# Batched matrix product: the last 2 MB load as two DMAs, and the first store waiting for the first of them

## The chip, the cores and the metric

The kernel runs on one NeuronCore of a Trainium2 chip. The metric is the device time of one execution in microseconds (us), the median of several executions. All DMAs of this kernel are issued by SyncE (SP), so they stand in one queue; TensorE (PE) multiplies, VectorE (DVE) casts the inputs to bf16, ScalarE (ACT) moves results out of PSUM, GpSimd (POOL) only waits at the end.

## The reference

```python
batch, m, k, n = 16, 512, 512, 512
a: (batch, k, m) float32      b: (batch, k, n) float32

def reference(a, b):
    return np.matmul(a.transpose(0, 2, 1), b).astype(np.float32)
```

Sixteen products of 512 x 512 matrices, the first of each stored transposed. The inputs are 33.55 MB, the output is 16.78 MB, and each byte crosses between HBM and SBUF once.

## The kernel before

**Tiling.** The 16 products are taken in 8 pairs. A load (one for a, one for b) brings a whole pair, 2 MB: the 128 partitions hold 64 partitions of each of the two products, and each partition holds R = 8 consecutive rows of its matrix, one contiguous run of 16 KB. Four such tiles (`x0` to `x3`, NX = 4) are used in rotation: load n goes into `x[n % 4]`, even n is a, odd n is b. The first pair is fetched in smaller pieces (256 KB, 768 KB, 1 MB for each of a and b). Counting by whole loads, the last two are n = 14 (a of pair 7) and n = 15 (b of pair 7).

**Casts.** DVE turns each tile into bf16 in two halves (v = 0 and v = 1, RV = 4 rows of each partition, tiles `abf0/1` and `bbf0/1`), line 109. For v = 0 it first waits until the load has landed (line 108, semaphore `s_x[n % 4]`). After the second half it raises `s_in`, which tells SP that the tile is free.

**Matmuls.** PE runs a loop over the pairs (line 136): for each half v, it waits for two casts and issues 32 matmuls into four PSUM tiles (line 147). ACT copies the finished PSUM tiles into an output tile `o` (line 172) and raises `s_out` once per pair (line 177). There are 7 output tiles for 8 pairs, so the results of nearly all pairs can stay in SBUF until they are stored.

**The order on SP.** SP's program is written out by hand, and an instruction that waits holds up everything behind it:

1. the six small loads of pair 0;
2. loads n = 2 to 15 (line 80); from n = 4 on each waits for `s_in`, that is, for the casts that free its tile;
3. line 83, a wait until load 14 has landed:

```python
n = 2 * pairs - 2
nc.sync.wait_ge(s_x[n % NX], 16 * (n // NX + 1))
```

4. the stores of pairs 0 to 6 (line 86), each behind a wait for `s_out` of its pair; 2 MB each, in runs of 8 KB (one partition and one of the two products);
5. after a barrier at the end of the block, the store of pair 7 (line 184).

So no store is issued until the loads are nearly over: the inputs stream in first, then the outputs stream out. POOL waits for the stores of pairs 0 to 6, and the program ends when the store of pair 7 has landed.

Of the kernel before, what the change touches and what calls it, by code (L numbers as in the profile page):

```python
# [8 lines left out]
def kernel(  # L9
# [6 lines left out]
    nc = tc.nc  # L16
# [11 lines left out]
    R = K // Q  # L28
    V = 2
    RV = R // V  # L30
    T = M // P
    H = T // 2
    pairs = batch // G
    in_v = [x.rearrange("(pair g) (q r) m -> pair (g q) r m", g=G, r=R) for x in (a, b)]
# [8 lines left out]
    NX = 4  # L43
# [10 lines left out]
    x_ts = [pool.tile([P, R, M], f32, name=f"x{j}") for j in range(NX)]  # L54
# [4 lines left out]

    s_x = [tc.alloc_semaphore(f"s_x{j}") for j in range(NX)]  # L60
    s_f = [tc.alloc_semaphore(f"s_f{j}") for j in range(2)]
    s_o0 = tc.alloc_semaphore("s_o0")
    s_o = tc.alloc_semaphore("s_o")
    s_in = tc.alloc_semaphore("s_in")
# [6 lines left out]
    with tc.tile_critical(no_gpsimd_drain=True):  # L71
# [5 lines left out]
        for n in range(2, 2 * pairs):  # L77
            if n >= NX:
                nc.sync.wait_ge(s_in, n - NX + 1)
            nc.sync.dma_start(x_ts[n % NX][:], in_v[n % 2][n // 2]).then_inc(s_x[n % NX], 16)  # L80

        n = 2 * pairs - 2
        nc.sync.wait_ge(s_x[n % NX], 16 * (n // NX + 1))
        for i in range(pairs - 1):
            nc.sync.wait_ge(s_out, i + 1)
            nc.sync.dma_start(out_v[i], o_ts[i % NO][:]).then_inc(s_o if i else s_o0, 16)
# [11 lines left out]
        for i in range(1, pairs):  # L98
            for v in range(V):
                if i == 1 and v == 0:  # L100
                    nc.vector.wait_ge(s_mm, G * H)
                if i > 1 and v == 0:
                    nc.vector.wait_ge(s_v, G * (i - 1))
                if i > 1 and v == 1:
                    nc.vector.wait_ge(s_mm, G * H * i)
                for n in (2 * i, 2 * i + 1):
                    if v == 0:
                        nc.vector.wait_ge(s_x[n % NX], 16 * (n // NX + 1))
                    nc.vector.tensor_copy(  # L109
                        out=(bbf_ts if n % 2 else abf_ts)[v][:],  # L110
                        in_=x_ts[n % NX][:, v * RV:(v + 1) * RV, :],
                    ).then_inc(s_cast, 1)
                    if v == V - 1:

                        nc.vector.memset(dve_done[:, n:n + 1], 0.0).then_inc(s_in, 1)  # L115
# [99 lines left out]
```

## Time and profile before

| quantity | value |
|---|---|
| median of 5 runs | 123.85 us (123.58 to 124.2) |
| the profiled execution's own time | 123.61 us |
| its span, first to last instruction | 121.9 us |
| PE busy | 63.6 us (52%) |
| DVE busy | 37.9 us (31%) |
| ACT busy | 32.2 us (26%) |
| one 2 MB load, issue to landing, median (a / b) | 12.1 / 15.9 us |
| one 2 MB store, issue to landing, median | 25.1 us |
| HBM read / written | 33.55 / 16.78 MB |

The time of the profiled execution is 1.7 us longer than its span, and 0.24 us shorter than the median. A 2 MB transfer that is issued into a full queue lands long after its issue, since it stands behind others: the last two rows but one are waiting times more than transfer times.

Besides the engines' instructions the trace holds a record of every DMA packet, with its start, its duration and its size. Packets of the 2 MB loads are 16 KB and take 611 ns each; packets of the stores are 8 KB and take 309 ns each. The packets run on 16 DMA engines (called rings below). When a DMA is through on a ring, the ring writes 4 bytes to its semaphore; the DMA has landed when all 16 of these writes are made.

### The profile page before, as it was taken

To read this page: it belongs to the slowest core of one execution; us is meant where nothing else is said; L and a number is where in the kernel's file an instruction comes from. 1 tells how busy PE (TensorE), PEld (TensorE's weight loads), DVE (VectorE), ACT (ScalarE), POOL (GpSimd) and SP (SyncE) were. 2 spreads that over 40 slices of the span, in tenths; PEclk is the share of its full clock that TensorE was granted. 3 is DMA by queue.
4 is the path that set the end of the run, shared out by engine and by line. 5 is a ranking of instruction groups with operands and counts; after the bars stand their busy time and mean duration, and the time that the engine had idled before them with its cause. 6 is when DMAs were issued, how large, how long until landed. Compare 5 with 4: busy or idle time off the path is not lost. (4 is left out here: it accounts for less than half of the span.)

```text
span 121.9 us, 1208 instructions
## 1 busy us (share of the span) xinstructions
PE 63.6 (52%) x480; PEld 35.7 (29%) x480; DVE 37.9 (31%) x48; ACT 32.2 (26%) x41; POOL 0.2 (0%) x4
## 2 busy tenths in 40 slices
PE   0006928739979659979919929936991000000000
PEld 0002403226546335636516606612550000000000
DVE  0052070294494091484265447419000000000000
ACT  4000330510660930190560380190048000000000
POOL 0000000000000000000000000000000000000000
PEclk9999995999999995999999999995899855555555
DMA  3999999999999999999999999999999999999994
GB/s 92 383 415 428 457 430 430 430 430 430 430 436 436 430 430 430 430 430 430 430 430 430 436 430 430 430 358 425 430 428 428 422 430 428 428 428 430 430 430 202
DMA packets 5056, 50.33 MB, mean 413 GB/s; under 512 B 448, under 2 KB 448, under 8 KB 960
## 3 DMA queue, kind: packets, MB, share of 16 engines
q1 hardware_dynamic: 5056, 50.33, 97.8%
HBM read 33.55 MB, written 16.78 MB: 413 GB/s over the span
## 5 line engine op out<-in xcount | busy, mean ns | idle before, releaser
L147 PE MATMUL ps<-bbf,abf 64*128 64x512 bf16 x448 | 52.8, 393 | 15.4 <-PEq L142 15.4
L147 PEld LDWEIGHTS ps<-bbf,abf 64*128 64x128 bf16 x448 | 31.7, 112 | 36.6 <-issue 22.0
L172 ACT COPY o<-ps 128x1024 f32<-128x1024 f32 x28 | 26.3, 1026 | 42.5 <-PE ps L147 42.5
L109 DVE CAST abf<-x 128x2048 bf16<-128x2048 f32 x14 | 17.1, 1224 | 17.2 <-PE ps L147 11.9
L109 DVE CAST bbf<-x 128x2048 bf16<-128x2048 f32 x14 | 17.1, 1224 | 16.7 <-DMA x<-in_b_dram 16.7
L127 PE MATMUL ps<-bbf,abf 128*128 128x512 bf16 x32 | 10.8, 512 | 12.8 <-PEq L125 12.8
L127 PEld LDWEIGHTS ps<-bbf,abf 128*128 128x128 bf16 x32 | 4.1, 133 | 19.0 <-issue 18.0
L166 ACT COPY o<-ps 128x1024 f32<-128x1024 f32 x4 | 4.1, 1013 | 18.4 <-PE ps L127 18.4
L93 DVE CAST abf<-x 128x2048 bf16<-128x2048 f32 x2 | 2.5, 1226 | 12.0 <-PE ps L127 6.1
L93 DVE CAST bbf<-x 128x2048 bf16<-128x2048 f32 x2 | 2.4, 1224 | 1.5 <-DMA x<-in_b_dram 1.5
L177 ACT ACTIVATE done<-done 1x1 uint32<-1x1 uint32 x8 | 1.6, 197 | 0.0
L166 ACT ACT_TABLE_LOAD x1 | 1.3, 1283 | 0.9 <-SPq L71 0.9
L115 DVE MEMSET done<- 1x1 f32 x14 | 0.8, 59 | 0.0
L97 DVE MEMSET done<- 1x1 f32 x2 | 0.1, 59 | 0.0
L199 POOL MEMSET const-bfloat16-1.0<- 128x1 bf16 x1 | 0.1, 103 | 0.0
L199 POOL MEMSET const-uint8-127<- 128x1 uint8 x1 | 0.1, 102 | 0.0
L199 POOL MEMSET const-float32-0.0<- 128x1 f32 x1 | 0.1, 100 | 0.2 <-issue 0.2
L199 POOL MEMSET const-float32-1.0<- 128x1 f32 x1 | 0.1, 99 | 0.0
## 6 DMA issues: line engine op xcount, KB each, us to landing
out_dram<-o SPq DMA_DIRECT2D x8, 2048.0 KB, 25.1
x<-in_a_dram SPq DMA_DIRECT2D x7, 2048.0 KB, 12.1
x<-in_b_dram SPq DMA_DIRECT2D x7, 2048.0 KB, 15.9
x<-in_a_dram SPq DMA_DIRECT2D x1, 1024.0 KB, 8.2
x<-in_b_dram SPq DMA_DIRECT2D x1, 1024.0 KB, 10.1
x<-in_a_dram SPq DMA_DIRECT2D x1, 768.0 KB, 4.4
x<-in_b_dram SPq DMA_DIRECT2D x1, 768.0 KB, 6.2
x<-in_a_dram SPq DMA_DIRECT2D x1, 256.0 KB, 2.7
```

What stands on the lines that cost most here:

```text
L93: nc.vector.tensor_copy(out=bf_ts[0][:], in_=x_ts[j][:, u * RV:(u + 1) * RV, :]).then_inc(s_cast, 1)
L97: nc.vector.memset(dve_done[:, j:j + 1], 0.0).then_inc(s_in, 1)
L109: nc.vector.tensor_copy(out=(bbf_ts if n % 2 else abf_ts)[v][:], in_=x_ts[n % NX][:, v * RV:(v + 1) * RV, :],).then_inc(s_cast, 1)
L115: nc.vector.memset(dve_done[:, n:n + 1], 0.0).then_inc(s_in, 1)
L127: mm = nc.tensor.matmul(ps_ts[0][h][:, t % 2, :], a_m[:, r, t], bbf_ts[0][:, r, :], start=(r == 0), stop=(r == RV - 1),)
L147: mm = nc.tensor.matmul(ps_ts[g][h][:, t % 2, :], a_m[:, t], bbf_ts[v][rows, r, :], start=(v == 0 and r == 0), stop=(v == V - 1 and r == R ...
L166: nc.scalar.copy(out=o_ts[0][:, g, 2 * h:2 * h + 2, :], in_=ps_ts[0][h][:]).then_inc(s_ev[h], 1)
L172: ev = nc.scalar.copy(out=o_ts[i % NO][:, g, 2 * h:2 * h + 2, :], in_=ps_ts[g][h][:])
L177: nc.scalar.memzero(act_done[:, i:i + 1]).then_inc(s_out, 1)
L199: nc = _bacc.Bacc("TRN2", target_bir_lowering=False, num_devices=1)
```

## The change

Load 15 is split into two DMAs of 1 MB. Each partition's 16 KB run becomes two of 8 KB: the first DMA brings rows 0 to 3 of each partition, which the cast v = 0 reads, and signals a new semaphore `s_h`; the second brings rows 4 to 7, which the cast v = 1 reads, and signals `s_x[3]`. SP waits for `s_h` in place of the landing of load 14 before it issues the first store. DVE waits for `s_h` before the first half-cast of load 15, and for `s_x[3]` before the second. Nothing else differs.

```diff
+    s_h = tc.alloc_semaphore("s_h")
...
-            nc.sync.dma_start(x_ts[n % NX][:], in_v[n % 2][n // 2]).then_inc(s_x[n % NX], 16)
-
-        n = 2 * pairs - 2
-        nc.sync.wait_ge(s_x[n % NX], 16 * (n // NX + 1))
+            src, x = in_v[n % 2][n // 2], x_ts[n % NX]
+            if n < 2 * pairs - 1:
+                nc.sync.dma_start(x[:], src).then_inc(s_x[n % NX], 16)
+            else:
+                nc.sync.dma_start(x[:, 0:RV, :], src[:, 0:RV, :]).then_inc(s_h, 16)
+                nc.sync.dma_start(x[:, RV:R, :], src[:, RV:R, :]).then_inc(s_x[n % NX], 16)
+
+        nc.sync.wait_ge(s_h, 16)
...
-                    if v == 0:
+                    last = n == 2 * pairs - 1
+                    if last and v == 0:
+                        nc.vector.wait_ge(s_h, 16)
+                    if last and v == 1 or not last and v == 0:
                         nc.vector.wait_ge(s_x[n % NX], 16 * (n // NX + 1))
```

## The prediction

> **What bounds the kernel now.** I read the page's slices first, then the DMA queue, then the waits of SP, then short windows around the step from loads to stores, and last the packet records there.
>
> ```profile
> span 121.9 us, 1208 instructions
> ...
> PE   0006928739979659979919929936991000000000
> ...
> DMA  3999999999999999999999999999999999999994
> GB/s 92 383 415 428 457 430 430 430 430 430 430 436 436 430 430 430 430 430 430 430 430 430 436 430 430 430 358 425 430 428 428 422 430 428 428 428 430 430 430 202
> ...
> q1 hardware_dynamic: 5056, 50.33, 97.8%
> ```
>
> The DMA engines are busy in every slice, 97.8% of the span in all, while PE stops two thirds of the way through. The kernel is one stream of packets: 78 us of loads, 39 us of stores, a start of 2 us and a tail of 1.3 us. The engines matter only where they keep the stream from being fed. The one slice that falls clearly short is the 27th, 358 GB/s, about 79 to 82 us: the step from loads to stores, where the change works.
>
> ```profile
> SPq L80 <- DVE done L115: 43.8, 10, 8.5
> SPq L210 <- DMA out_dram<-o: 26.4, 1, 26.4
> ...
> SPq L86 <- DMA x<-in_a_dram: 10.6, 1, 10.6
> SPq L86 <- ACT done L177: 3.2, 1, 3.2
> ```
>
> In this view of SP's waits (line, who is waited for, us, times, longest) the third row is the wait that the change replaces: SP holds the first store until load 14 has landed.
>
> ```profile
> 12.00:78.00 66.00, 50.78 (x392) 29.42 (x392) 31.73 (x41) 23.24 (x30) 0.00 (x0) 0.95 1.01 432
> 78.50:81.50 3.00, 1.87 (x18) 0.95 (x14) 0.00 (x0) 2.85 (x4) 0.00 (x0) 1.00 0.93 350
> 82.00:120.00 38.00, 8.53 (x64) 4.28 (x64) 3.25 (x5) 4.29 (x7) 0.00 (x0) 0.65 1.01 428
> ```
>
> In these windows the last figure is GB/s: 432 in the loads, 428 in the stores, 350 for 3 us between. At 430 that stretch would carry (430 - 350) x 3.0 = 240 KB more, 0.56 us of streaming. The semaphore writes give the loss more sharply. On the mean of the 16 rings, fourteen whole loads end 4.86 us apart, the stores 4.90, but load 15 ends 5.23 after load 14: 0.37 us lost. On the ring that is last, load 14 ends at 76.28 and load 15 at 81.37, 5.09 apart: 0.22 lost. The packets show where: the 16 KB packets that begin between 78.7 and 79.9 take up to 1,138 ns for 611. None is lost later: the first 8 KB store packet of a ring follows its last load packet at once, 80.94 on the earliest ring, and takes 309 ns like all others.
>
> **The change part by part**, against the profiled execution (span 121.9, time 123.61; the median is 0.24 above it, and I add the sum to the median).
>
> Two halves for one load: 8 packets of 16 KB per ring become 16 of 8 KB. The row for 8 KB loads is in the first pair, whose two 1 MB halves end 2.45 us apart; two are 4.90 for 4.86: +0.04 us.
>
> One more issue on SP: an issue of a whole load lasts 0.33 us, and the last begins at 65.63. The second half would be issued by 66.3, and its data are due 2.45 us after 76.28, so 12 us of queued loads cover it. Without that cover it would cost its 0.33 us.
>
> DVE and what follows: the first half-cast of load 15 begins at 81.75, 0.38 us after the landing. With the first half landing at 76.28 + 2.45 = 78.73 it can begin at about 79.1; the second half lands about 81.2, close to where the whole did. PE's last pair can then start up to 2.5 us sooner than 83.27, and the last store be issued up to that much before 94.11. This is worth nothing: that store's packets start only when six stores have drained, at 120.57 - 4.90 = 115.7. If the last pair came late instead, the cover is 115.7 - 94.11, some 21 us.
>
> The later wait: this is the term that decides.
>
> ```profile
> 76.60 12.48 SPq L86 DMA_DIRECT2D out_dram<-o  x7
> ...
> L86 SPq DMA_DIRECT2D out_dram<-o x7: 403/560/5146, 76.6 to 84.5; - x7
> ```
>
> These are the timeline and the line's own view (duration in ns, shortest, median, longest). The first store is issued at 76.60, 0.32 after load 14's last semaphore write; the sixth takes 5.1 us because the queue takes no more. After the change SP waits for 78.73 and issues at 78.73 + 0.32 = 79.05, 2.45 later. All seven stores of line 86, the barrier and the store of line 184 stand behind that wait. Five stores then go out at about 0.56 us each, far faster than the 4.9 us in which one drains, so all depends on whether the first is in time.
>
> When do the rings run dry? Without any slowdown they end the second half one load after load 14: 75.71 + 4.90 = 80.62 on the first ring, 81.18 on the last. From issue to a store's first packet there is no direct row, since all stores so far were issued into a full queue.
>
> The bound below is the kernel's first load, issued into empty rings at 0.94: its first packets begin between 1.96 and 2.25, so 1.02 to 1.31. The store would be there at 80.07 to 80.36, before any ring runs dry: no gap. The bound above is the first store itself: issued at 76.60, and the first packets of load 15 that take longer begin between 78.75 and 79.27, 2.15 to 2.67 later. If that is the moment when a store's work reaches the rings, it now does so at 81.20 to 81.72, after they have run dry. A dry ring also has to fill again: the first two packets of the kernel take 0.27 us more than 2 x 84 ns on the mean of the rings. The first store then runs at full rate from 81.47 to 81.99, where before it did on the last ring from 81.37: +0.10 to +0.62 us.
>
> I take the upper bound. It is the same kind of DMA at the same place in the stream, while the first load is another kind at another place. The end of the kernel is set by the last ring, so I take the upper part of the 0.10 to 0.62 and say +0.50. The slowdown goes with it, for the loads would be over before a store touches them; that is in the sum already, which compares with 81.37. The 0.04 lies before the dry spell. Sum: 123.85 + 0.50 = 124.35.
>
> Two rules of the Trainium skill bear on this. "DMA: Bandwidth & Descriptors", section "Bandwidth", gives 341 GB/s for a 1 MB load (one issued by GpSimd) and wants no smaller ones; by it the two halves would cost 2 x 1.05 MB / 341 = 6.1 us for 4.9, an estimate of +1.3, 125.1 us. The trace's halves, which stand in a stream of others, show no such loss. The same page, section "Latency and other measured facts", puts the first byte of a DMA issued by SP at about 0.6 us after issue; by that the store would be in time at 79.7, and the sum would be no worse than +0.04, 123.9.
>
> **The rivals.**
>
> *Seamless, and nothing comes of it.* The store arrives as quickly as the first load did. For it: the rows of the first load, and 0.3 to 1.1 us of margin. The slowdown either stays, since its cause (store reads beside the last load writes) is only moved, +0.04; or it goes on the last ring, 0.04 - 0.22 = -0.18. 123.67 to 123.9.
>
> *Seamless, and the slowdown goes on all rings* (faster). For it: it is the only loss in the stream, it comes after the stores are issued, and only there. On the mean of the rings it is 0.37, by the windows 0.56; less 0.04 it is 0.33 to 0.52, and the time 123.33 to 123.52, say 123.43. Against it: the last ring loses only 0.22, and all rings must be finished. But the profiled execution is 0.24 shorter than the median, and a longer slowdown in ordinary ones would fit that.
>
> *The slowdown stays and the gap is added* (slower). The stores reach the rings late, the last rings still write loads and are slowed by 0.22 to 0.37, and the dry ones fill up behind: +0.62 + 0.37 = +1.0, 124.85. It decides as soon as the way from issue to packet is over 2.1 us (81.18 - 79.05). Against it: overlap and gap can hardly both be long on one ring.
>
> **How the numbers follow.** About 0.3% (0.37 us) is what a measurement of this kernel can tell from no change. The forecast, a gap, has 0.50; its own range is +0.10 to +0.80, 123.95 to 124.65, and I give 0.43 of it to slower and 0.07 to same. Seamless without effect has 0.19: 0.16 same, 0.03 faster. Seamless with gain has 0.24: 0.23 faster, 0.01 same. Gap and slowdown has 0.07, slower. Together faster 0.26, same 0.24, slower 0.50. The time is that of the forecast, 124.35. The range leaves out the tips of the two outer cases: 123.4 to 124.95.
>
> **What would show it.** A gap: in the profile after, the slice near 81 us falls below 358 GB/s, and a window of half a microsecond there carries less than the 197 of 80.00 to 80.50 before; load packets stay at 611 or 309 ns to their end, and the first store packets begin later than 81.4. Seamless: the stores' packets follow the second half without a break, and then either some of its packets are long (no effect) or none (gain). The halves are right if they end 2.45 us apart. The forecast is wrong if the first store packet begins less than 1.6 us after its issue, for then no ring runs dry; the chances are wrong if anything outside 78 to 83 us moves the end.

## The result, and the profile after

| | before | after |
|---|---|---|
| median, many runs of both | 123.93 us (86 runs) | 123.61 us (44 runs) |
| ratio, 95% interval | | 0.9965 [0.9954, 0.9977] |
| the profiled execution's own time | 123.61 us | 123.73 us |
| its span | 121.9 us | 122.0 us |

By the ratio the kernel is faster by 0.35%, some 0.43 us; the two medians lie 0.32 us apart. The forecast was slower by 0.50 us: it was wrong.

The page's slices and its DMA queue, after:

```profile
span 122.0 us, 1209 instructions
...
PE   0006919289989949829969928989900000000000
...
DMA  3999999999999999999999999999999999999993
GB/s 98 373 429 430 470 430 430 430 430 430 430 430 430 430 430 430 430 430 430 430 430 430 430 430 419 419 424 430 427 427 430 427 430 430 430 430 424 430 430 132
...
q1 hardware_dynamic: 5200, 50.33, 97.6%
```

The 27th slice, 358 GB/s before, now has 424. The step from loads to stores can hardly be seen any more. The 144 packets more are 128 for the halved load and 16 semaphore writes.

SP's waits after (line, who is waited for, us, times, longest), then the timeline around the step (start, duration, engine, line, operation):

```profile
SPq L83 <- DVE done L123: 43.5, 9, 9.0
SPq L218 <- DMA out_dram<-o: 26.6, 1, 26.6
...
SPq L91 <- DMA x<-in_b_dram: 12.6, 1, 12.6
```

```profile
79.38 10.09 SPq L91 DMA_DIRECT2D out_dram<-o  x7
79.39 1.23 DVE L117 CAST bbf<-x 128x2048 bf16<-128x2048 f32 x1 [0.87 <-DMA x<-in_b_dram]
...
81.06 7.21 PE L155 MATMUL ps<-bbf,abf 64*128 64x512 bf16 x64 [0.35 <-PEq L150]
...
90.72 3.64 SPq L192 DMA_DIRECT2D out_dram<-o  x1
```

SP now waits for a piece of b, and the first store is issued at 79.38, 2.78 us later than before. The cast of the first half begins at once, PE's last pair 2.2 us sooner, and the last store is issued 3.4 us sooner.

```profile
12.00:78.00 66.00, 51.88 (x391) 28.91 (x391) 31.59 (x41) 23.22 (x30) 0.00 (x0) 0.92 1.01 431
78.50:81.50 3.00, 2.65 (x27) 1.46 (x23) 2.00 (x3) 2.51 (x3) 0.00 (x0) 1.00 1.01 429
82.00:120.00 38.00, 6.27 (x58) 3.68 (x54) 1.12 (x2) 4.62 (x7) 0.00 (x0) 0.64 1.01 426
```

These are the windows of the prediction on the kernel after, the last figure GB/s again. The middle one carries 429 where it carried 350. A part of that difference comes from how such a window counts; the experiment with the late store alone shows how much.

The packet records say the same without the windows' edges. Times are in us. A load ends on a ring with its semaphore write; "last ring" is the latest of the 16 writes, and "load 15 after load 14" the time from one end to the next:

```
                                          before   after
load 14 ends, last ring                    76.28   76.60
load 15 after load 14, mean of the rings    5.23    4.91  (2.45 + 2.45)
load 15 after load 14, last ring            5.09    4.91
the 8 stores, last ring                    39.20   39.20
from the last packet to the span's end      1.30    1.27
```

No packet of the halves takes longer than 309 ns, and the first store packets follow without a break, from 80.55 on: 1.17 us after their issue. No ring ran dry. That the profiled execution after is nevertheless 0.12 longer is the first row: its last ring was 0.32 later from the start of the kernel on, which took back the 0.18 won at the step. One ring's late start is carried through to the end, and it differs from execution to execution; so the gain must be read from the many runs.

### The profile page after: what moved, and what is told of

Same layout as the page of the kernel before. It is cut to its first block, busy times and chain, and to the rows that moved or that the text cites. A ratio compares the mean times of both kernels' runs of the same rounds, so it can differ in the third digit from the quotient of the medians.

```text
span 122.0 us, 1209 instructions
## 1 busy us (share of the span) xinstructions
PE 63.5 (52%) x480; PEld 35.4 (29%) x480; DVE 38.2 (31%) x48; ACT 32.1 (26%) x41; POOL 0.2 (0%) x4
## 4 chain that ended last, share of the span: by engine, by line
DMA 59%; DVE 6%; issue 3%; ACT 3%; SPq 3%; ACTq 0%
DMA x<-in_b_dram 53%; DMA out_dram<-o 6%; ACT o L180 3%; DVE bbf L117 3%; DVE abf L117 3%; SPq L77 1%; SPq L75 1%; SPq L74 1%; SPq L83 0%; DVE done L123 0%; ACTq L72 0%; SPq L218 0%; SPq L72 0%
## 5 line engine op out<-in xcount | busy, mean ns | idle before, releaser
L155 PE MATMUL ps<-bbf,abf 64*128 64x512 bf16 x448 | 54.5, 401 | 11.8 <-PEq L150 11.8
L135 PE MATMUL ps<-bbf,abf 128*128 128x512 bf16 x32 | 9.0, 444 | 13.0 <-PEq L133 13.0
```

What stands on the lines that cost most here:

```text
L135: mm = nc.tensor.matmul(ps_ts[0][h][:, t % 2, :], a_m[:, r, t], bbf_ts[0][:, r, :], start=(r == 0), stop=(r == RV - 1),)
L155: mm = nc.tensor.matmul(ps_ts[g][h][:, t % 2, :], a_m[:, t], bbf_ts[v][rows, r, :], start=(v == 0 and r == 0), stop=(v == V - 1 and r == R ...
```

## The experiments

All are compared with the kernel before on the same chip. Two theories were to be told apart at first: that the later issue of the first store makes the gain, and that the smaller packets do. Then: what it is in an early issue that slows the loads.

**The split alone.** The changed kernel, with the wait of before:

```diff
-        nc.sync.wait_ge(s_h, 16)
+        n = 2 * pairs - 2
+        nc.sync.wait_ge(s_x[n % NX], 16 * (n // NX + 1))
```

> Load 15 in two halves, but the first store is issued as before, after load 14 has landed (about 76.6 us). If the gain comes from the later issue alone, the last load's packets are slowed as in the profile of before (load 15 ends about 5.2 us after load 14 on the mean of the rings, in place of 4.90) and the time is that of before plus 0.04: ratio about 1.000. If the gain comes from the smaller packets of the halves, none is slowed and the ratio is that of the change, 0.9965.

Ratio 1.0022 [0.9998, 1.0045]; load 15 ends 5.19 us after load 14 on the mean of the rings (5.02 on the last), and 35 of its 8 KB packets take 333 to 605 ns for 309. The window in its profile:

```profile
78.50:81.50 3.00, 2.65 (x27) 1.49 (x24) 2.22 (x2) 2.76 (x4) 0.00 (x0) 1.00 1.00 385
```

385 GB/s for the 429 after. The halves are slowed as the whole was: the split by itself gains nothing.

**The late store alone**, with load 15 in one piece; the wait is for matmuls that end at about the right time:

```diff
-        n = 2 * pairs - 2
-        nc.sync.wait_ge(s_x[n % NX], 16 * (n // NX + 1))
+        nc.sync.wait_ge(s_mm, G * H * (pairs - 2) + G)
```

> Load 15 in one piece, but the first store waits for the matmuls that finish the first half of pair 6's results, about 78.7 us, so it is issued about 2.2 us later than before. If the later issue alone makes the gain: no packet of load 15 is slowed, it ends 4.86 us after load 14, ratio 0.996. If the packet size makes it: slowed as before, 5.2 us, ratio 1.000.

The profile is clear: the first store is issued at 78.67, load 15 takes 4.86 us on the mean of the rings and on the last, and no packet is slowed. The time is not: 0.9999 [0.9984, 1.0015]. In these runs the kernel before had a median of 123.62 us, 0.3 lower than in the first comparison, and the changed kernel did not run beside it. So both were run side by side, twice, once on another chip and once on this one. The five expectations are, in order, for the changed kernel, the late store alone and the kernel before in the first round, and for the changed kernel and the late store alone in the second.

> The changed kernel once more, beside the next three on one chip. If its gain is the slowdown's removal: ratio 0.996 to 0.998, no packet of load 15 slowed. If the gain depends on the chip, as the 0.9999 of the late store alone would allow, it is nearer 1.000 here.

> The unsplit load with the late store, on the same chip as the changed kernel. If the late issue is the whole of the gain: the same ratio as the changed kernel within 0.001 (0.04 us better by the larger packets). If the split has a part in it: 1.000 here, and 0.996 to 0.997 for the changed kernel.

> The kernel before against itself: ratio 1.000 within the interval, which shows what the method can tell. Its profile is a second look at the slowdown: load 15 ends 5.2 us (mean of the rings) after load 14 if the first was typical; if the slowdown varies, another value between 4.9 and 5.6.

> The changed kernel beside the late store alone, once more, on one chip. The slowdown costs the last ring 0.2 to 0.5 us in the two profiles of before, so ratio 0.996 to 0.999.

> The unsplit load with the late store. If the late issue is the whole of the gain: within 0.001 of the changed kernel. If the split has a part in it: 1.000, and the changed kernel 0.996 to 0.997.

The changed kernel came to 0.9986 [0.9965, 1.0007] and 0.9979 [0.9952, 1.0006], the late store alone to 0.9989 [0.9964, 1.0014] and 0.9967 [0.9939, 0.9995]. Side by side they agree within 0.0012, and in none of the four profiles is a packet of load 15 slowed. So the split is not needed for the gain, as far as intervals of 0.002 to 0.003 can tell; a part of it smaller than that stays open.

The size of the gain is known less well than the packets suggest. The middle values of the changed kernel's two repeats are gains of 0.17 and 0.26 us, where the first comparison gave 0.43, and of the four intervals only the last leaves out 1. The chip is not what hid the late store's gain the first time, for the 0.9967 was measured on the same chip as the 0.9999. What hid it stays open. The kernel before against itself came to 1.0 [0.9976, 1.0024]. In its second profile the slowdown is there again, 5.26 us on the mean and 5.34 on the last ring: the last ring lost 0.48 where the first profile showed 0.22.

The late store's window in its first profile holds a warning:

```profile
78.50:81.50 3.00, 1.86 (x18) 0.93 (x14) 0.00 (x0) 2.86 (x4) 0.00 (x0) 1.00 0.93 396
```

396 GB/s, though every packet there took its 611 or 309 ns. The windows, like the slices, count all bytes of a packet where it starts, and the 16 rings start their 16 KB packets in clumps; a window of 3 us can be off by some 8% for that alone. If each packet is counted by the part of it that lies in the window, this one carries 430 GB/s, and the 350 of the kernel before become 377. Then (430 - 377) x 3.0 = 159 KB are missing, or 0.37 us: the same loss as by the semaphore writes.

**No wait at all**, so that five stores are queued directly behind load 15:

```diff
-        n = 2 * pairs - 2
-        nc.sync.wait_ge(s_x[n % NX], 16 * (n // NX + 1))
```

> Without the wait the stores of pairs 0 to 4 go into the queue right behind load 15, at about 66 us. If the slowdown comes when store reads follow the last load reads in a ring that still writes loads, it depends on the order in the ring and not on the time of issue: about the same as before, 5.2 us for load 15, ratio 1.000. If it comes from the burst of five issues, about 2 to 3.5 us after it, it moves to 68 to 70 us and load 15 itself is not slowed; the ratio is 1.000 again, but the slow packets are in another load.

Ratio 1.0033 [1.0014, 1.0053]. The stores are issued from 67.78 on:

```profile
66.26 0.33 SPq L80 DMA_DIRECT2D x<-in_a_dram  x1
67.41 0.33 SPq L80 DMA_DIRECT2D x<-in_b_dram  x1
67.78 22.98 SPq L84 DMA_DIRECT2D out_dram<-o  x7
```

No packet is slowed in the 11 us that follow. The slow ones begin at 79.06, six of them, all in load 15: 4.96 us on the mean, 5.18 on the last ring. So they do not come a fixed time after the issue; they come before the loads end. This profile is of an execution of 125.51 us, 1.6 above the kernel's median, and its last ring is 1.70 behind the mean from the first whole load on. Why the ratio is above 1, with less lost on the mean of the rings than before (0.10 us for 0.37), was not found.

**One early store**: the first is issued as before, the second only when load 15 has landed.

```diff
         for i in range(pairs - 1):
+            if i == 1:
+                nc.sync.wait_ge(s_x[(2 * pairs - 1) % NX], 16 * ((2 * pairs - 1) // NX + 1))
             nc.sync.wait_ge(s_out, i + 1)
```

> Only the first store is issued after load 14; the second waits until load 15 has landed. If the burst of issues slows the loads, one store does no harm: load 15 ends 4.86 us after load 14, ratio 0.996. If the first store's own reads beside the last load writes do, the slowdown is as before: 5.2 us, ratio 1.000.

Ratio 1.0022 [1.0002, 1.0042]. In its profile load 15 takes 5.58 us on the mean and 6.05 on the last ring, with 36 slow packets of up to 1,208 ns:

```profile
78.50:81.50 3.00, 3.00 (x31) 1.74 (x29) 1.23 (x1) 0.89 (x1) 0.00 (x0) 1.00 0.92 306
```

One store is enough; the burst of five issues is not the cause. How much is lost is another matter: this execution took 124.98 us, 1.15 above its kernel's median, so the 6.05 need not be usual.

**A quarter in place of a half**, in the changed kernel: the first DMA brings rows 0 and 1, the second rows 2 to 7, and both casts of load 15 wait for the whole.

```diff
-                nc.sync.dma_start(x[:, 0:RV, :], src[:, 0:RV, :]).then_inc(s_h, 16)
-                nc.sync.dma_start(x[:, RV:R, :], src[:, RV:R, :]).then_inc(s_x[n % NX], 16)
+                nc.sync.dma_start(x[:, 0:RV // 2, :], src[:, 0:RV // 2, :]).then_inc(s_h, 16)
+                nc.sync.dma_start(x[:, RV // 2:R, :], src[:, RV // 2:R, :]).then_inc(s_x[n % NX], 16)
...
-                    if last and v == 1 or not last and v == 0:
+                    if v == 0:
```

> The first of the two DMAs brings a quarter of load 15 in place of a half (rows 0 and 1 of each partition), so the first store is issued at about 77.8 us, between the 76.6 of before and the 79.05 of the change; the casts of load 15 wait for the whole. If store packets do harm when they are in the rings while the rings still have loads to read (2 us before the loads end, about 78.7): still slowed, load 15 in all 5.0 to 5.3 us, ratio 0.999 to 1.001. If it is enough to be 1 us later: 4.90 us, ratio 0.996 to 0.998.

The first store is issued at 78.15, and from 77.1 on no packet of load 15 is slowed: to be issued about 1 us later than before is enough. But the ratio is 1.0029 [1.0005, 1.0053]. Two parts of this are in the profile: load 15 takes 5.01 us on the mean and 5.09 on the last ring, so that the last ring loses as much as it did before. Its 8 packets of 4 KB and 8 of 12 KB take 0.09 more than 8 of 16 KB at their usual 159, 460 and 611 ns, and twelve of the 4 KB packets, begun between 76.67 and 77.09 and so before the store was issued, take up to 340 ns; and the program ends 1.52 us after its last packet, 1.27 to 1.33 in all others. Where the second comes from was not tried.

**The first store behind the whole of load 15**, in one piece, so that the rings must run dry:

```diff
-        n = 2 * pairs - 2
+        n = 2 * pairs - 1
```

> Load 15 in one piece and the first store behind the landing of the whole of it, so the rings must run dry: this measures the way from issue to first packet. By the forecast's upper bound it is 2.15 to 2.67 us and the dry spell 2.5 to 3.0 with the 0.32 from landing to issue: ratio 1.018 to 1.024. By the lower bound it is 1.0 to 1.3: 1.3 to 1.6 us dry on the last ring, less the 0.2 to 0.5 of the slowdown that goes: ratio 1.007 to 1.011.

Ratio 1.0081 [1.0053, 1.011]. The dry spell that the forecast expected of the change can be seen here. SP's timeline, then windows of half a microsecond:

```profile
81.81 9.62 SPq L86 DMA_DIRECT2D out_dram<-o  x7
```

```profile
80.00:80.50 0.50, 0.50 (x8) 0.31 (x6) 0.00 (x0) 0.08 (x1) 0.00 (x0) 1.00 0.99 426
80.50:81.00 0.50, 0.50 (x8) 0.32 (x6) 0.00 (x0) 0.50 (x1) 0.00 (x0) 1.00 0.09 33
81.00:81.50 0.50, 0.50 (x8) 0.25 (x5) 0.00 (x0) 0.50 (x2) 0.00 (x0) 1.00 0.00 0
81.50:82.00 0.50, 0.50 (x6) 0.12 (x2) 0.19 (x1) 0.50 (x1) 0.00 (x0) 1.00 0.00 0
82.00:82.50 0.50, 0.13 (x2) 0.00 (x0) 0.50 (x1) 0.50 (x2) 0.00 (x0) 1.00 0.00 0
82.50:83.00 0.50, 0.00 (x0) 0.00 (x0) 0.50 (x2) 0.50 (x1) 0.00 (x0) 1.00 0.61 262
```

The store is issued at 81.81 and its first packets begin, ring by ring, between 82.73 and 82.88: 0.92 to 1.07 us. That is the number that the prediction had no row for.

**A store in the middle of the loads**: the first is issued between loads 14 and 15, so that the rings pass from loads to stores twice.

```diff
             nc.sync.dma_start(x_ts[n % NX][:], in_v[n % 2][n // 2]).then_inc(s_x[n % NX], 16)
+            if n == 2 * pairs - 2:
+                nc.sync.wait_ge(s_out, 1)
+                nc.sync.dma_start(out_v[0], o_ts[0][:]).then_inc(s_o0, 16)
...
-        for i in range(pairs - 1):
+        for i in range(1, pairs - 1):
```

> The first store is issued between loads 14 and 15, so the rings pass from loads to stores twice. If the slowdown belongs to each such step with the store already queued: long packets at the end of load 14 (about 75 us) and again at the end of load 15, each 0.2 to 1.2 us on the last ring: ratio 1.002 to 1.008. If it belongs to the end of the load stream alone: one slow stretch, ratio 1.000.

Ratio 1.0034 [1.0003, 1.0066]. Load 14, now followed by a store, takes 5.26 us on the mean and 5.22 on the last ring for 4.86; load 15, followed by the other stores, 4.96 and 5.27. Its windows before the first step, at it, and among the last stores:

```profile
60.00:73.00 13.00, 9.63 (x88) 5.88 (x84) 6.40 (x9) 7.64 (x10) 0.00 (x0) 1.00 1.02 437
73.50:76.00 2.50, 2.50 (x26) 1.62 (x24) 1.68 (x4) 0.00 (x0) 0.00 (x0) 1.00 0.96 347
...
88.00:118.00 30.00, 8.72 (x64) 4.32 (x64) 2.57 (x5) 3.82 (x5) 0.00 (x0) 0.67 1.01 428
```

Slow packets begin at 73.96 (29 of them, up to 994 ns), and most of a second, smaller group from 83.86 on. Each step from loads to an already queued store costs its own slowdown; the step back, from the store to load 15, costs nothing (the store takes 4.92).

Together, with the time of the first store's issue:

```
                   issue   load 15 after 14,   slow     ratio [95%]
                           mean / last ring    packets
before             76.60   5.23 / 5.09         yes      -
before, again      77.07   5.26 / 5.34         yes      1.0    [0.9976, 1.0024]
split alone        76.69   5.19 / 5.02         yes      1.0022 [0.9998, 1.0045]
one early store    76.95   5.58 / 6.05         yes      1.0022 [1.0002, 1.0042]
no wait            67.78   4.96 / 5.18         yes      1.0033 [1.0014, 1.0053]
quarter            78.15   5.01 / 5.09         no       1.0029 [1.0005, 1.0053]
late alone         78.67   4.86 / 4.86         no       0.9999 [0.9984, 1.0015]
late alone, again  79.18   4.86 / 4.86         no       0.9989 [0.9964, 1.0014]
late alone, third  79.33   4.86 / 4.86         no       0.9967 [0.9939, 0.9995]
after              79.38   4.91 / 4.91         no       0.9965 [0.9954, 0.9977]
after, again       79.01   4.91 / 4.90         no       0.9986 [0.9965, 1.0007]
after, third       79.19   4.91 / 4.90         no       0.9979 [0.9952, 1.0006]
whole load 15      81.81   4.86 / 4.86, dry    no       1.0081 [1.0053, 1.011]
```

A packet of load 15 is slowed in every profile where a store was queued by 77.1, and in none where it was issued from 78.15 on, but for the quarter's 4 KB packets, which were slow before any store was issued. The slow packets begin 1.9 to 2.8 us before the first ring ends its loads (80.86 to 80.97 in the five). The runs do not show what in a DMA engine does this. A reading that fits all of them is that a ring reads ahead of what it writes: a store that is there when the ring has issued its last load reads is read beside the last load writes, and one that comes later is not. It was not tested by itself, and it does not say why the loss differs so much, from 0.10 to 0.72 us on the mean of the rings.

## Why the prediction was wrong

**The step that failed** is the way from the first store's issue to its first packet. The prediction held two bounds, 1.02 to 1.31 us from the kernel's first load and 2.15 to 2.67 from the first slowed packets of load 15, and took the upper one for its +0.50, because it was "the same kind of DMA at the same place in the stream". Measured, the way is 0.92 to 1.07. The upper bound was no latency at all: without the wait such slow packets came 11.3 us after the issue. An event that follows another once, in one profile, had been read as caused by it with a delay. The prediction's own test, a first store packet less than 1.6 us after its issue, went against it: 1.17 us in the profile after.

**The dry spell** follows the same way. With 79.05 + 0.92 to 1.07 the store is there at 79.97 to 80.12, ahead of the 80.62 at which the first ring was to run dry. The first-load row, from another DMA at another place, was the right one to within 0.3 us. The refill of 0.27 us was mis-sized as well: in the kernel that does run dry, the first store packet of each ring takes 307 to 309 ns, as in a full stream, and the third 329 to 353; the first store takes 5.04 us on the mean of the rings for 4.90, so the refill is about 0.14.

**The rival that came true** is the seamless one with a gain, priced at 0.33 to 0.52 us; 0.43 was measured, but 0.17 and 0.26 in the repeats, so that the price was met so well is in part luck. Its argument was that the loss is longer in ordinary executions than on the last ring of the profiled one. The second profile of before fits it, 0.48 on the last ring for 0.22; two profiles do not show what is usual. Of the 0.56 from the windows, 0.19 come from counting packets where they start; the 0.37 from the semaphore writes was sound.

**The Trainium skill's rules.** The page "DMA: Bandwidth & Descriptors" spoke for the right side with its first byte about 0.6 us after issue (section "Latency and other measured facts"), though the store's first packet is measured at 0.92 to 1.07 from the start of the issue. Its 341 GB/s for a 1 MB load issued by GpSimd (section "Bandwidth") is not what halves in a full queue show: each half took 2.45 us, 428 GB/s.

**What was right**: the halves end 2.45 us apart, +0.04 us in all; the added issue on SP costs nothing; the sooner casts and matmuls are worth nothing (the last store is issued 3.4 us sooner, and its packets still stand behind the seven stores ahead); SP sees a landing 0.32 to 0.33 us after the last semaphore write; and the place, the step from loads to stores.

**Slips that moved nothing**: the loads take about 79 us and not 78 (2 + 79 + 39 + 1.3 make the span); the last store's packets start when seven stores have drained, not six; and the stores after the first do not go out at 0.56 us each in the changed kernel but, at the median, at 1.30, still faster than one drains.

## What to carry to other kernels

In a kernel that is one stream of transfers, look at the step from loads to stores packet by packet: here a store queued too early slowed the last loads, and one queued too late left the rings dry. An issue 3.8 us before the first ring's last load packet ended was too early and 2.6 us was not; the latest that was tried without a dry spell is 1.17, and by the 0.92 to 1.07 above about 1.1 would be the limit. The worth was small, 0.14 to 0.35% of the time in the three comparisons of the changed kernel. Measure the way from issue to first packet with one run in which the queue is made to run dry; do not take it from two events that happen to follow one another. Compare the ends of whole transfers, and not bytes in short windows, before a loss of some tenths of a microsecond is believed.

## What was not expected of the hardware

The 16 rings do not wait for one another: one that starts late stays late. In the first profile of the changed kernel the last ring is 0.69 us behind the mean after the first whole load, 0.69 after load 14 and 0.67 at the end. At load 14 the last ring was 0.2 to 1.7 us behind the mean (76.19 for 75.95 in another profile of the changed kernel, 78.07 for 76.37 in the one without the wait), and the end of the kernel moved with it. A dry spell set them level: with the first store behind the whole of load 15 the rings came in 0.95 us apart and went out 0.17 apart, which paid back a part of the 2.0 us that the mean ring stood still.
